# Queries and keys ordered by head, and differential scores over 64 rows of the array

## Chip, cores and metric

The kernel runs on one core of a Trainium2 chip. The metric is the device time of one execution in microseconds, the median of several runs. A profiled execution stands beside them; its times come from the hardware profiler.

## What is computed

A two-layer causal decoder trunk over 256 tokens of width 2048, in fp32. Layer 0 has a pooling mixer and a memory attention, then a squared-ReLU MLP. Then keys k1, k2 and values are made once from the residual stream, and layer 1 runs a differential attention with 12 heads: two query maps and two key maps of 64 channels for each head, and values of 128 channels.

```python
q1, q2 = (partial_rope(rms_norm(t, q_norm), cos, sin) for t in (q1, q2))   # (1, 256, 12, 64) each
a = softmax(mask(q1 @ k1.T * 64 ** -0.5)) - lam * softmax(mask(q2 @ k2.T * 64 ** -0.5))
o = a @ v                                                                  # a head: (256, 128)
token_out = rms_norm(o, subln_norm) * (1.0 - lam_init)
```

Beside it stand a memory attention of 4 heads of 128 channels, one output projection, and a second MLP.

## The kernel before

Activations lie with the channels on the 128 partitions, in 16 chunks (`NK`), and 256 tokens along the free dimension. Every large matmul is made in fp32r with operands split into a high and a low part. `Feed` brings the weights from DRAM in the order of their use, in blocks of 128x128, four to a "quad" of 512 columns. It loads them into `raw` (SyncE's queue), rounds a quad to its high part on ScalarE (`hi_ring<-raw`, L168) and takes the low part on VectorE (`lo_ring`, L169), three jobs ahead (`AHEAD`) of the matmul that needs it. The order is not written by hand: `program` is run twice, first dry, so that `Plan` collects the blocks in order, and then for real. The host lays the weights out in that order.

`b_tile` makes the query and key projections. For each of 16 chunks, `wide_step` takes one quad of 512 output columns and makes six matmuls (L449 to L451, three for each half of the tokens) with the tokens as rows of the result. After each wide step `tick()` runs what `at(d, fn)` put d ticks ahead; so the steps of the heads are laid between the projections' matmuls. The framework's scheduler then fixes each engine's order, and may shift an instruction against its neighbours.

A block of 128 columns is two heads of one map. The keys take `w_kv`'s blocks as they stand, six of map 0 and then six of map 1. The queries' chunk c, 512 columns of `w_in_q` as the host reorders them, has four heads: the first two heads' block of map 0 and of map 1, then the other two heads' blocks. `key_rows` and `query_rows` copy a projection out of PSUM (L490, L512), sum its squares by head, and `rope` turns the first 16 channels of each head in place. `turn_rows` transposes keys into `kT` (12 chunks of 128 x 256, six for each map, in the tile `big`). `turn_queries` transposes a pair of heads and evicts them (L1260) into two tiles of `qb`: in the first tile only partitions 0 to 63 are filled, in the second only 64 to 127. The rest was set to zero (L1249, L1250) once. So a score matmul can use all 128 rows of a key chunk, which holds two heads: the other head's 64 rows meet zeros.

`diff_head` is a head's attention, in four steps at ticks of their own:
- `scores`: for the second half of the queries (t = 1) both maps against 256 keys into `s1` (L1292), then for the first half both maps against 128 keys into `s0` (L1295). Both tiles are one PSUM bank of the tag "s", which has two. VectorE adds the causal mask (L1297, L1298), takes the maxima (L1302) and multiplies them by the row scales `y` (L1303). ScalarE makes the exponentials with their sums (L1306). VectorE combines the two maps into `a` (L1312 and the helper `stt`, L318).
- `turn`, four ticks later: three transposes of `a` (`dt`, L1321), and ScalarE's copy.
- `pv`: the product with the values (`do`, L1327 to L1329), its statistics and scale.
- `back`: transposes of the result (`o_t`, L1350) into `cat1`.

The heads of the last chunk run while `c_tile` makes the memory queries (`mq`, L429 to L431). The memory heads' scores use the same tag "s". The trace names the parts of one large tile alike: q, e, a and the rest are `att`, and `kT` and the values are `big`.

Of the kernel before, what the change touches and what calls it, by code (L numbers as in the profile page):

```python
# [9 lines left out]

F32 = mybir.dt.float32
F32R = mybir.dt.float32r
BF16 = mybir.dt.bfloat16
AF = mybir.ActivationFunctionType
ALU = mybir.AluOpType
AX = mybir.AxisListType
# [2 lines left out]
P = 128  # L19
# [86 lines left out]
class Feed:  # L106
# [119 lines left out]
    def quad(self, what):  # L226

        job = ("N", self.pos // 4)
        if self.dry:
            self.plan.entries.append(what)  # L230
            if self.pos % 4 == 0:
                self.plan.jobs.append(job)
            return Nothing(), Nothing()
        if self.pos % 4 == 0:
            self.fill(job)
        return self.split[job][:2]
# [44 lines left out]
def program(ctx, tc, plan, dry, xT, memT, par, lam, cst, wst, yT):  # L281
# [173 lines left out]
    def b_tile(ps, w, l, c, xs):  # L455
        for k in range(NK):
            wide_step(ps, (w, l, k, c, 4), xs, k)


    def rstd_from(name):  # L460
        st = stat("st_" + name)
# [22 lines left out]
    def key_rows(ps, cols, d):  # L484

        n = 512 // d
        raw = tp.tile([P, 2, 512], F32, tag="rows", bufs=3, name="krow")
        v = tp.tile([P, 2, n], F32, tag="w16", bufs=6, name="kv")
        for t in range(2):
            nc.scalar.activation(raw[:, t, :], ps[t], AF.Copy, scale=cols[0][:, t : t + 1])  # L490
            sq = tp.tile([P, 512], F32, tag="rowsq", bufs=1, name="ksq")
            nc.scalar.activation(sq, raw[:, t, :], AF.Square)
            nc.vector.tensor_reduce(
                out=v[:, t, :], in_=sq.rearrange("p (h d) -> p h d", d=d), axis=AX.X, op=ALU.add
            )
        v = v.rearrange("p t n -> p (t n)")
        nc.vector.tensor_scalar(out=v, in0=v, scalar1=1.0 / d, scalar2=EPS, op0=ALU.mult, op1=ALU.add)
        y = tp.tile([P, 2 * n], F32, tag="w16", bufs=6, name="ky")
        rsqrt_cols(y, v)
        for t in range(2):  # L500
            rows = raw[:, t, :].rearrange("p (h d) -> p h d", d=d)
            yb = y[:, t * n : t * n + n].unsqueeze(2).to_broadcast([P, n, d])
            nc.vector.tensor_mul(rows, rows, yb)
        return raw

    def query_rows(ps, cols, d):

        raw = tp.tile([P, 2, 512], F32, tag="rows", bufs=3, name="qrow")
        n = 512 // d
        v = tp.tile([P, 2 * n], F32, tag="w16", bufs=6, name="qv")  # L510
        for t in range(2):
            nc.scalar.copy(raw[:, t, :], ps[t])  # L512
            sq = tp.tile([P, 512], F32, tag="rowsq", bufs=1, name="qsq")
            nc.scalar.activation(sq, raw[:, t, :], AF.Square, scale=d ** -0.5)
            nc.vector.tensor_reduce(
                out=v[:, n * t : n * t + n], in_=sq.rearrange("p (h d) -> p h d", d=d),
                axis=AX.X, op=ALU.add,
            )
            nc.vector.tensor_scalar(
                out=v[:, n * t : n * t + n], in0=v[:, n * t : n * t + n],  # L520
                scalar1=cols[1][:, t : t + 1], scalar2=EPS, op0=ALU.mult, op1=ALU.add,
            )
        return raw, v
# [666 lines left out]
    at(12, lambda: c1.extend(columns("x")))  # L1190
    for c in range(3):
        ps = pair_of_banks(c, "k1")
        b_tile(ps, "w_kv", 0, c, x_kv)
        rows = key_rows(ps, c1, 64)
        rope(rows, ktab)
        for i in range(2):
            at(
                9,
                lambda i=i, c=c, rows=rows: turn_rows(
                    rows, 2 * i, kT[:, 4 * c + 2 * i : 4 * c + 2 * i + 2, :], gcol(G_KN)  # L1200
                ),
            )
# [40 lines left out]
    ab = [carve(384) for _ in range(2)]  # L1243
    aTb = [carve(384) for _ in range(2)]

    qb = [[carve(512).rearrange("p (m t) -> p m t", m=2) for _ in range(2)] for _ in range(3)]
    em1 = carve(512).rearrange("p (a t) -> p a t", a=2)
    for pair in qb:
        nc.vector.memset(pair[0][64:128], 0.0)  # L1249
        nc.vector.memset(pair[1][0:64], 0.0)  # L1250

    def turn_queries(rows, i, pair):
        t4 = pp.tile([P, 2, T], F32, tag="t", bufs=1, name="tq")
        for c in range(2):
            for t in range(2):
                nc.tensor.transpose(
                    t4[:, c, t * P : t * P + P], rows[:, t, (i + c) * P : (i + c) * P + P], ident
                )
        for g, r in enumerate((slice(0, 64), slice(64, 128))):
            nc.scalar.activation(pair[g][r], t4[r], AF.Copy, scale=qcol[r])  # L1260


    gsub = cp.tile([P, 1], F32, name="gsub")
    nc.vector.tensor_scalar_mul(gsub, gcol(G_SUB), 1.0 - LAM_INIT)
    idb = cp.tile([P, P], BF16, name="idb")
    nc.vector.tensor_copy(idb, ident)
    mkb = cp.tile([P, P], BF16, name="mkb")
    nc.vector.tensor_copy(mkb, const[:, C_MASK : C_MASK + P])

    def diff_head(h, q, y, lag, pv_lag, back_lag, by_pe):  # L1270

        j = h // 2
        e1, e0, a, aT = e1b[h % 2], e0b[h % 2], ab[h % 2], aTb[h % 2]
        yh = y.rearrange("p (t j m h) -> p t j m h", t=2, j=2, m=2)[:, :, j % 2, :, h % 2]
        ez = tp.tile([P, 2], F32, tag="ez", bufs=6, name="ez")

        def scores():
            s1 = pp.tile([P, 2, T], F32, tag="s", bufs=2, name="s1")
            s0 = pp.tile([P, 2, P], F32, tag="s", bufs=2, name="s0")
            if by_pe:  # L1280
                for m in range(2):
                    kk = kT[:, 6 * m + j, :]
                    nc.tensor.matmul(s1[:, m, :], q[:, m, P:T], kk, start=True, stop=False)
                    nc.tensor.matmul(s1[:, m, P:T], idb, mkb, start=False, stop=True)
                for m in range(2):
                    kk = kT[:, 6 * m + j, 0:P]
                    nc.tensor.matmul(s0[:, m, :], q[:, m, 0:P], kk, start=True, stop=False)
                    nc.tensor.matmul(s0[:, m, :], idb, mkb, start=False, stop=True)
            else:
                for m in range(2):  # L1290
                    kk = kT[:, 6 * m + j, :]
                    nc.tensor.matmul(s1[:, m, :], q[:, m, P:T], kk, start=True, stop=True)  # L1292
                for m in range(2):
                    kk = kT[:, 6 * m + j, 0:P]
                    nc.tensor.matmul(s0[:, m, :], q[:, m, 0:P], kk, start=True, stop=True)  # L1295
                mask = const[:, C_MASK : C_MASK + P].unsqueeze(1).to_broadcast([P, 2, P])
                nc.vector.tensor_add(s1[:, :, P:T], s1[:, :, P:T], mask)  # L1297
                nc.vector.tensor_add(s0, s0, mask)  # L1298
            mx = tp.tile([P, 2, 2], F32, tag="m4", bufs=6, name="mx")
            z = tp.tile([P, 2, 2], F32, tag="m4", bufs=6, name="z")  # L1300
            for t, s in ((1, s1), (0, s0)):
                nc.vector.tensor_reduce(out=mx[:, t, :], in_=s, axis=AX.X, op=ALU.max, negate=True)  # L1302
            nc.vector.tensor_mul(mx, mx, yh)  # L1303
            for t, s, e in ((1, s1, e1), (0, s0, e0)):
                for m in range(2):
                    nc.scalar.activation(  # L1306
                        e[:, m, :], s[:, m, :], AF.Exp, bias=mx[:, t, m : m + 1],
                        scale=yh[:, t, m : m + 1], accum_out=z[:, t, m : m + 1],
                    )

            zr = tp.tile([P, 2], F32, tag="m2", bufs=12, name="zr")
            nc.vector.reciprocal(zr, z[:, :, 1])  # L1312
            stt(zr, zr, nlam, z[:, :, 0], ALU.mult, ALU.mult)
            stt(ez, z[:, :, 0], EPS, z[:, :, 0], ALU.mult, ALU.mult)
            for t, e, dst in ((1, e1, a[:, P : P + T]), (0, e0, a[:, 0:P])):
                stt(dst, e[:, 1, :], zr[:, t : t + 1], e[:, 0, :], ALU.mult, ALU.add)
# [7 lines left out]
        def pv():  # L1324
# [3 lines left out]
            nc.tensor.matmul(o[:, 1, :], aT[:, P:T], vv[:, 0, hs], start=True, stop=False)  # L1328
            nc.tensor.matmul(o[:, 1, :], aT[:, T : T + P], vv[:, 1, hs], start=False, stop=True)  # L1329
            osb = vt("osb").rearrange("p (a b) -> p a b", a=2)  # L1330
            if by_pe:
                nc.vector.tensor_copy(osb, o)
                o = osb
            ss = tp.tile([P, 2], F32, tag="m2", bufs=12, name="o_ss")
            junk = vt("o_sq")
            for t in range(2):
# [21 lines left out]

    for c in range(3):
        ps = pair_of_banks(0, "q1")  # L1360
        b_tile(ps, "w_in_q", 1, c, x_mx)
        rows, v = query_rows(ps, c1, 64)
        rope(rows, qtab)
        y = query_scale(v, c1)
        for i in range(2):
# [3 lines left out]
            for g in range(2):  # L1369
                h = 2 * i + g  # L1370

                diff_head(
                    2 * j + g, q[g], y, 6 + 4 * h, *((8, 4 if c == 0 else 3) if c < 2 else (7, 3)), False
                )
    pT1 = tp.tile([P, 2, T], F32R, tag="acc2", bufs=1, name="pT1")
    pT1_lo = tp.tile([P, 2, T], F32R, tag="rowsq", bufs=1, name="pT1_lo")
# [101 lines left out]
```

## Time and profile before

| | |
|---|---|
| median of 3 runs | 2037.37 us (2037.07 to 2037.41) |
| profiled execution | 2036.78 us, its span 2035.0 us |
| TensorE matmuls busy | 2030.0 us, 11068 records |
| VectorE / ScalarE busy | 1722.7 / 1352.4 us |
| granted TensorE clock | 1.000 |
| HBM read | 386.54 MB, 191 GB/s over the span |

The span runs from the first to the last instruction; the profiled execution's own time has 1.78 us around it. A matmul's record lasts from its start until its result is written, so records overlap; how fast they follow each other is seen from their ends, as in the chain of waits. PE names the matmuls, PEld the weight loads, DVE is VectorE and ACT is ScalarE.

### The profile page before, as it was taken

The page shows a single profiled execution, that of the slowest core. Times are in us where ns is not written, and L with a number is a line of the kernel's source. Part 1 is how long each engine was busy: PE and PEld are TensorE (multiplying, and loading weights), DVE is VectorE, ACT ScalarE, POOL GpSimd, SP SyncE. Part 2 cuts the span into 40 slices and gives each one's busy share as a digit, 9 for nine tenths or more (in the row PEclk, how much of TensorE's full clock was granted, in tenths as well). Part 3 has the DMA queues.
Part 4 walks back from the last instruction along what each step waited for, and adds up shares of the span by engine and source line. Part 5 has one row for each costly group of instructions (what it writes and reads, how often), then busy time and mean ns, then how long its engine had stood idle before and what let it go on. Part 6 is the DMA issues. An engine that isn't in the chain of part 4 may idle for free.

```text
span 2035.0 us, 32279 instructions
## 1 busy us (share of the span) xinstructions
PE 2030.0 (100%) x11068; PEld 1753.2 (86%) x11068; DVE 1722.7 (85%) x3226; ACT 1352.4 (66%) x2520; POOL 54.5 (3%) x67
## 2 busy tenths in 40 slices
PE   9999999999999999999999999999999999999999
PEld 8888888888888888888888889888888888888888
DVE  8888889889879878999766788989879978988997
ACT  7765577666656756778665688566667656766764
POOL 0001300000000000000000000410000000000000
PEclk9999999999999999999999999999999999999999
DMA  9566556555555555645565434556555555555564
GB/s 317 167 200 191 189 177 203 190 197 197 187 202 201 186 205 193 212 168 186 189 227 195 166 125 140 192 177 204 189 197 197 186 202 195 188 208 200 195 205 134
DMA packets 110630, 390.75 MB, mean 192 GB/s; under 512 B 12544, under 2 KB 15232, under 8 KB 110464
## 3 DMA queue, kind: packets, MB, share of 16 engines
q1 hardware_dynamic: 110240, 388.61, 56.6%
q8 instruction: 86, 1.41, 0.3%
q14 instruction: 80, 0.66, 0.1%
q10 hardware_dynamic: 224, 0.07, 0.0%
HBM read 386.54 MB, written 2.10 MB: 191 GB/s over the span
## 4 chain that ended last, share of the span: by engine, by line
PE 99%; DMA 0%; DVE 0%; SPq 0%; ACT 0%; issue 0%; ACTq 0%
PE x_bank L415 33%; PE x_bank L417 16%; PE wo L415 6%; PE p L798 5%; PE p L799 5%; PE p L800 5%; PE wo L417 3%; PE u L415 2%; PE ff L415 2%; PE u L417 1%; PE q L449 1%; PE q L451 1%; PE k L449 1%; PE q L450 1%; PE k L450 1%; PE v L450 1%
## 5 line engine op out<-in xcount | busy, mean ns | idle before, releaser
L168 ACT CAST hi_ring<-raw 128x512 fp32r<-128x512 f32 x1193 | 736.0, 620 | 513.8 <-PE x_bank L415 303.3
L169 DVE TENSOR_TENSOR lo_ring<-raw,hi_ring 128x512 fp32r<-128x512 f32 x1193 | 817.7, 696 | 187.9 <-ACT hi_ring L168 149.3
L415 PE MATMUL x_bank<-fx,hi_ring 128*128 128x512 f32 x1920 | 602.2, 395 | 0.0
L417 PEld LDWEIGHTS x_bank<-fx,lo_ring 128*128 128x128 f32 x1920 | 361.1, 188 | 83.5
L417 PE MATMUL x_bank<-fx,lo_ring 128*128 128x256 f32 x1920 | 377.5, 278 | 0.0
L415 PEld LDWEIGHTS x_bank<-fx,hi_ring 128*128 128x128 f32 x1920 | 301.4, 189 | 9.3
L415 PE MATMUL x_bank<-z,hi_ring 128*128 128x512 f32 x960 | 301.1, 395 | 0.0
L169 DVE TENSOR_TENSOR lo_ring<-slab,hi_ring 128x1024 fp32r<-128x1024 f32 x188 | 230.0, 1224 | 54.5 <-ACT hi_ring L168 53.7
L168 ACT CAST hi_ring<-slab 128x1024 fp32r<-128x1024 f32 x188 | 196.8, 1047 | 73.3 <-PE x_bank L415 36.4
L417 PEld LDWEIGHTS x_bank<-z,lo_ring 128*128 128x128 f32 x960 | 180.5, 188 | 41.7
L417 PE MATMUL x_bank<-z,lo_ring 128*128 128x256 f32 x960 | 188.8, 278 | 0.0
L415 PE MATMUL wo<-cat,hi_ring 128*128 128x512 f32 x512 | 162.5, 398 | 0.0
L415 PEld LDWEIGHTS x_bank<-z,hi_ring 128*128 128x128 f32 x960 | 151.9, 189 | 6.4 <-ACT room L722 0.4
L417 PEld LDWEIGHTS wo<-cat,lo_ring 128*128 128x128 f32 x512 | 95.6, 188 | 20.9
L722 ACT COPY room<-x_bank 128x512 f32<-128x512 f32 x180 | 104.8, 582 | 2.0 <-PE x_bank L417 2.0
L417 PE MATMUL wo<-cat,lo_ring 128*128 128x256 f32 x512 | 102.5, 280 | 0.0
L798 PE MATMUL p<-hi_ring,sit 128*128 128x512 f32 x256 | 100.5, 393 | 0.0
L799 PE MATMUL p<-hi_ring,sit 128*128 128x512 f32 x256 | 100.2, 392 | 0.0
L800 PE MATMUL p<-lo_ring,sit 128*128 128x512 f32 x256 | 99.7, 390 | 0.0
L767 ACT ACTIVATE room<-room 128x256 f32<-128x256 f32 x128 | 53.2, 415 | 41.2 <-DVE room L318 40.9
L415 PEld LDWEIGHTS wo<-cat,hi_ring 128*128 128x128 f32 x512 | 79.0, 189 | 1.3 <-DVE cat L318 0.4
L798 PE MATMUL p<-hi_ring,z 128*128 128x512 f32 x192 | 75.2, 392 | 0.0
(336 smaller groups left out, 3128.0 us busy)
## 6 DMA issues: line engine op xcount, KB each, us to landing
raw<-in_w SPq DMA_DIRECT2D x595, 512.0 KB, 3.9
slab<-in_w SPq DMA_DIRECT2D x124, 512.0 KB, 3.5
memraw<-in_mem SPq DMA_DIRECT2D x5, 512.0 KB, 3.9
resid<-in_x SPq DMA_DIRECT2D x8, 256.0 KB, 5.5
room<-in_w SPq DMA_DIRECT2D x4, 512.0 KB, 4.6
out_y<-resid SPq DMA_DIRECT2D x15, 128.0 KB, 1.9
memraw<-in_mem SPq DMA_DIRECT2D x5, 256.0 KB, 5.7
raw<-in_w SPq DMA_DIRECT2D x3, 256.0 KB, 3.2
```

The lines of the kernel that those rows point to most:

```text
L168: self.last_cast = self.nc.scalar.copy(hi, src)
L169: low = self.nc.vector.tensor_sub(lo, src, hi.bitcast(F32))
L415: nc.tensor.matmul(ps, hi, xs[:, k, :], start=first and c == 0, stop=False)
L417: nc.tensor.matmul(ps[:, T : 2 * T], lo, xs[:, k, 0:T], start=False, stop=last and c == len(ks) - 1,)
L449: nc.tensor.matmul(ps[t], x[t][1], hi, start=k == 0, stop=False)
L450: nc.tensor.matmul(ps[t], x[t][0], hi, start=False, stop=False)
L451: nc.tensor.matmul(ps[t], x[t][0], lo, start=False, stop=k == NK - 1)
L722: nc.scalar.copy(x, ps)
L767: at(3, lambda: nc.scalar.activation(stage[i % 8], y[:, 0:T], AF.Square))
L798: nc.tensor.matmul(ps, a[1], hi, start=first, stop=False)
L799: nc.tensor.matmul(ps, a[0], hi, start=False, stop=False)
L800: nc.tensor.matmul(ps, a[0], lo, start=False, stop=last)
```

## The change

Blocks of weights for queries and keys are taken in another order: a chunk of 512 columns now has the four heads of map 0 in its first half and those of map 1 in the second (`map_tile` in place of `b_tile`). The copy out of PSUM writes the rows by head: 64 channels of map 0, then 64 of map 1, so that a block of 128 columns is one head with both its maps. The keys' chunk h is then head h, map 0 in partitions 0 to 63 and map 1 in 64 to 127, and so are the queries; the zero halves go, with their zeroing and with one of the two evictions of a pair.

The scores are matmuls over 64 rows, from partition 0 for map 0 and from partition 64 for map 1. Their order takes turns between the maps. The PSUM tiles are now one for each map, with three blocks of 128 columns: the first half of the queries in block 0, the second half in blocks 1 and 2. Masks and maxima go by map. The maximum comes in three columns, and one more small operation joins two of them. The branch `by_pe`, which no call used, goes with its two constants.

```diff
+    def map_tile(ps, w, l, blocks, xs):
+        for k in range(NK):
+            wide_step(ps, [(w, l, k, n, 1) for n in blocks], xs, k)
+
+    def by_head(row, d):
+        return row if d == P else row.rearrange("p (h m d) -> p m h d", m=2, d=d)
+
+    def by_map(row, d):
+        return row if d == P else row.rearrange("p (m h d) -> p m h d", m=2, d=d)
...
-            nc.scalar.copy(raw[:, t, :], ps[t])
+            nc.scalar.copy(by_head(raw[:, t, :], d), by_map(ps[t], d))
...
-        b_tile(ps, "w_kv", 0, c, x_kv)
+        map_tile(ps, "w_kv", 0, (2 * c, 2 * c + 1, 6 + 2 * c, 7 + 2 * c), x_kv)
...
-    qb = [[carve(512).rearrange("p (m t) -> p m t", m=2) for _ in range(2)] for _ in range(3)]
+    qb = [carve(512).rearrange("p (c t) -> p c t", c=2) for _ in range(3)]
-    for pair in qb:
-        nc.vector.memset(pair[0][64:128], 0.0)
-        nc.vector.memset(pair[1][0:64], 0.0)
...
-        for g, r in enumerate((slice(0, 64), slice(64, 128))):
-            nc.scalar.activation(pair[g][r], t4[r], AF.Copy, scale=qcol[r])
+        nc.scalar.activation(q, t4, AF.Copy, scale=qcol)
...
-            s1 = pp.tile([P, 2, T], F32, tag="s", bufs=2, name="s1")
-            s0 = pp.tile([P, 2, P], F32, tag="s", bufs=2, name="s0")
...
-                for m in range(2):
-                    kk = kT[:, 6 * m + j, :]
-                    nc.tensor.matmul(s1[:, m, :], q[:, m, P:T], kk, start=True, stop=True)
-                for m in range(2):
-                    kk = kT[:, 6 * m + j, 0:P]
-                    nc.tensor.matmul(s0[:, m, :], q[:, m, 0:P], kk, start=True, stop=True)
-                mask = const[:, C_MASK : C_MASK + P].unsqueeze(1).to_broadcast([P, 2, P])
-                nc.vector.tensor_add(s1[:, :, P:T], s1[:, :, P:T], mask)
-                nc.vector.tensor_add(s0, s0, mask)
+            s = [pp.tile([P, 3, P], F32, tag="s", bufs=2, name=f"s{m}") for m in range(2)]
+            for m, t in ((0, 0), (1, 1), (0, 1), (1, 0)):
+                r = slice(64 * m, 64 * m + 64)
+                nc.tensor.matmul(
+                    s[m][:, t : 2 * t + 1, :], q[r, t * P : t * P + P], kT[r, h, 0 : t * P + P],
+                    start=True, stop=True,
+                )
+            mask = const[:, C_MASK : C_MASK + P].unsqueeze(1).to_broadcast([P, 2, P])
+            mx3 = tp.tile([P, 2, 3], F32, tag="m6", bufs=4, name="mx3")
+            for m in range(2):
+                nc.vector.tensor_add(s[m][:, 0:3:2, :], s[m][:, 0:3:2, :], mask)
+                nc.vector.tensor_reduce(
+                    out=mx3[:, m, :], in_=s[m], axis=AX.X, op=ALU.max, negate=True
+                )
+            nc.vector.tensor_tensor(
+                out=mx3[:, :, 1], in0=mx3[:, :, 1], in1=mx3[:, :, 2], op=ALU.min
+            )
-            for t, s in ((1, s1), (0, s0)):
-                nc.vector.tensor_reduce(out=mx[:, t, :], in_=s, axis=AX.X, op=ALU.max, negate=True)
-            nc.vector.tensor_mul(mx, mx, yh)
+            nc.vector.tensor_mul(mx, mx3[:, :, 0:2].rearrange("p m t -> p t m"), yh)
...
-        b_tile(ps, "w_in_q", 1, c, x_mx)
+        map_tile(ps, "w_in_q", 1, (4 * c, 4 * c + 2, 4 * c + 1, 4 * c + 3), x_mx)
```

More of the change, by code (lines that the diff above doesn't have):

```diff
@@ L12 @@
 F32R = mybir.dt.float32r
-BF16 = mybir.dt.bfloat16
 AF = mybir.ActivationFunctionType
@@ L229, in quad @@
         if self.dry:
-            self.plan.entries.append(what)
+            self.plan.entries += what if isinstance(what, list) else [what]
             if self.pos % 4 == 0:
@@ L489, in key_rows @@
         for t in range(2):
-            nc.scalar.activation(raw[:, t, :], ps[t], AF.Copy, scale=cols[0][:, t : t + 1])
+            nc.scalar.activation(
+                by_head(raw[:, t, :], d), by_map(ps[t], d), AF.Copy, scale=cols[0][:, t : t + 1]
+            )
             sq = tp.tile([P, 512], F32, tag="rowsq", bufs=1, name="ksq")
@@ L1244, in program, with turn_queries @@
     aTb = [carve(384) for _ in range(2)]
-    qb = [[carve(512).rearrange("p (m t) -> p m t", m=2) for _ in range(2)] for _ in range(3)]
+    qb = [carve(512).rearrange("p (c t) -> p c t", c=2) for _ in range(3)]
     em1 = carve(512).rearrange("p (a t) -> p a t", a=2)
-    for pair in qb:
-        nc.vector.memset(pair[0][64:128], 0.0)
-        nc.vector.memset(pair[1][0:64], 0.0)
-    def turn_queries(rows, i, pair):
+    def turn_queries(rows, i, q):
         t4 = pp.tile([P, 2, T], F32, tag="t", bufs=1, name="tq")
@@ L1258, in turn_queries @@
                 )
-        for g, r in enumerate((slice(0, 64), slice(64, 128))):
-            nc.scalar.activation(pair[g][r], t4[r], AF.Copy, scale=qcol[r])
+        nc.scalar.activation(q, t4, AF.Copy, scale=qcol)
     gsub = cp.tile([P, 1], F32, name="gsub")
     nc.vector.tensor_scalar_mul(gsub, gcol(G_SUB), 1.0 - LAM_INIT)
[L1265 to L1268, printed above, removed]
@@ L1270, in diff_head @@
-    def diff_head(h, q, y, lag, pv_lag, back_lag, by_pe):
-        j = h // 2
+    def diff_head(h, q, y, lag, pv_lag, back_lag):
         e1, e0, a, aT = e1b[h % 2], e0b[h % 2], ab[h % 2], aTb[h % 2]
-        yh = y.rearrange("p (t j m h) -> p t j m h", t=2, j=2, m=2)[:, :, j % 2, :, h % 2]
+        yh = y.rearrange("p (t h m) -> p t h m", t=2, m=2)[:, :, h % 4, :]
         ez = tp.tile([P, 2], F32, tag="ez", bufs=6, name="ez")
         def scores():
-            s1 = pp.tile([P, 2, T], F32, tag="s", bufs=2, name="s1")
-            s0 = pp.tile([P, 2, P], F32, tag="s", bufs=2, name="s0")
-            if by_pe:
-                for m in range(2):
-                    kk = kT[:, 6 * m + j, :]
-                    nc.tensor.matmul(s1[:, m, :], q[:, m, P:T], kk, start=True, stop=False)
-                    nc.tensor.matmul(s1[:, m, P:T], idb, mkb, start=False, stop=True)
-                for m in range(2):
-                    kk = kT[:, 6 * m + j, 0:P]
[L1287 to L1295, printed above, removed]
-                mask = const[:, C_MASK : C_MASK + P].unsqueeze(1).to_broadcast([P, 2, P])
-                nc.vector.tensor_add(s1[:, :, P:T], s1[:, :, P:T], mask)
-                nc.vector.tensor_add(s0, s0, mask)
@@ L1299, in scores @@
+            for m in range(2):
[5 more added lines that the diff above has]
+                out=mx3[:, :, 1], in0=mx3[:, :, 1], in1=mx3[:, :, 2], op=ALU.min
+            )
             mx = tp.tile([P, 2, 2], F32, tag="m4", bufs=6, name="mx")
+            nc.vector.tensor_mul(mx, mx3[:, :, 0:2].rearrange("p m t -> p t m"), yh)
@@ L1300, in scores @@
             z = tp.tile([P, 2, 2], F32, tag="m4", bufs=6, name="z")
-            for t, s in ((1, s1), (0, s0)):
-                nc.vector.tensor_reduce(out=mx[:, t, :], in_=s, axis=AX.X, op=ALU.max, negate=True)
-            nc.vector.tensor_mul(mx, mx, yh)
-            for t, s, e in ((1, s1, e1), (0, s0, e0)):
+            for t, e in ((1, e1), (0, e0)):
                 for m in range(2):
                     nc.scalar.activation(
-                        e[:, m, :], s[:, m, :], AF.Exp, bias=mx[:, t, m : m + 1],
+                        e[:, m, :], s[m][:, t : 2 * t + 1, :].rearrange("p a b -> p (a b)"), AF.Exp, bias=mx[:, t, m : m + 1],
@@ L1330, in pv @@
             osb = vt("osb").rearrange("p (a b) -> p a b", a=2)
-            if by_pe:
-                nc.vector.tensor_copy(osb, o)
-                o = osb
             ss = tp.tile([P, 2], F32, tag="m2", bufs=12, name="o_ss")
@@ L1372, in program @@
                 diff_head(
-                    2 * j + g, q[g], y, 6 + 4 * h, *((8, 4 if c == 0 else 3) if c < 2 else (7, 3)), False
+                    2 * j + g, q[:, g, :], y, 6 + 4 * h, *((8, 4 if c == 0 else 3) if c < 2 else (7, 3))
                 )
```

## The prediction, on record before the result

> **What bounds the kernel now.** I read the page first, then the busy time by stage, then the chain of waits around one head's scores.
>
> ```profile
> span 2035.0 us, 32279 instructions
> PE 2030.0 (100%) x11068; PEld 1753.2 (86%) x11068; DVE 1722.7 (85%) x3226; ACT 1352.4 (66%) x2520; POOL 54.5 (3%) x67
> PE 99%; DMA 0%; DVE 0%; SPq 0%; ACT 0%; issue 0%; ACTq 0%
> ...
> core 0: us, PE busy (x) PEld busy (x) DVE busy (x) ACT busy (x) POOL busy (x), PEclk, DMA share, GB/s
> ...
> 1149.00:1205.00 56.00, 56.00 (x306) 48.08 (x305) 46.25 (x149) 45.55 (x137) 0.00 (x0) 1.00 0.40 131
> 1205.00:1260.00 55.00, 54.97 (x418) 52.22 (x417) 49.24 (x170) 48.56 (x155) 0.00 (x0) 1.00 0.39 129
> ```
>
> TensorE is busy for 2030.0 of 2035.0 us and is 99% of the chain that ended last. The second view is the stage that the change is about, 1149 to 1260 us: TensorE idles there for 0.03 us in all, at a granted clock of 1.00. So the program's time is TensorE's list of instructions, and an edit counts only if it makes that list shorter or longer, or if it makes TensorE wait. VectorE (46.25 of 56, then 49.24 of 55) and ScalarE (45.55, 48.56) are over 80% busy here, so a wait is not far off.
>
> **The scores on TensorE.** One head, in the chain of waits:
>
> ```profile
> 1165.11 0.33 PE dt L1321 x3
> 1165.44 0.87 PE s L1292 x4
> 1166.30 0.45 PE s L1295 x4
> 1166.75 0.23 PE q L449
> 1166.98 0.23 PE q L450
> ...
> L1292 PEld LDWEIGHTS s<-big,att x48: 188/191/193, 1149.6 to 1245.8; 128*128 128x128 f32 x48
> L1292 PE MATMUL s<-big,att x48: 377/379/383, 1149.9 to 1246.1; 128*128 128x256 f32 x48
> ...
> L1295 PEld LDWEIGHTS s<-big,att x48: 187/192/193, 1150.5 to 1250.5; 128*128 128x128 f32 x48
> L1295 PE MATMUL s<-big,att x48: 270/275/351, 1150.7 to 1250.6; 128*128 128x128 f32 x48
> ```
>
> Columns of the first rows are start, length, line. The two fp32 matmuls of 256 columns (L1292) leave four records in 0.87 us, the two of 128 columns (L1295) four in 0.45: each fp32 matmul runs as two records, each with its own weight load. A head's scores cost 0.87 + 0.45 = 1.32 us, and twelve heads 15.8 us, 0.78% of the program. Half of each array pass multiplies zeros, since 64 of q's 128 rows are the other head's.
>
> After the change the eight records stay, with the same columns, but each uses 64 rows, and the rows take turns: map 0 (128 columns), map 1 (256), map 0 (256), map 1 (128). If different halves run at once, the bound is half of 1.32, or 0.66. Nearer is the weight load, which the change does not shorten in columns:
>
> ```profile
> 1226.31 0.65 PE s L1292 x3
> 1226.95 0.34 PE st_mq L596 x4
> ...
> 1229.55 0.52 PE s L1295 x4
> ```
>
> L596 multiplies 128x128 weights by only two columns, and its records still end 0.11 us apart (0.34 us in three steps; the first ends with the record before it). So loads pass at one per 0.11 us, and eight take 0.88 us. I take 0.88, because every row here has loads in line: a gain of 1.32 - 0.88 = 0.44 us for a head whose four matmuls stand together. The ends are 0 (the halves run in line) and 0.66.
>
> They do not stand together in all heads. The order on an engine is laid by the framework's scheduler, and before the change five of the twelve heads have something between their score matmuls (the heads scored at 1197.82, 1215.30, 1225.92, 1235.51 and 1245.41); the rows of the first and the last:
>
> ```profile
> 1197.82 0.60 PE L1292 MATMUL s<-big,att 128*128 128x256 f32 x2
> 1198.39 0.52 PE L1321 MATMUL dt<-const,att 128*128 128x128 f32 x3
> 1198.75 0.60 PE L1292 MATMUL s<-big,att 128*128 128x256 f32 x2
> ...
> 1245.41 1.03 PE L1292 MATMUL s<-big,att 128*128 128x256 f32 x4
> ...
> 1250.28 0.61 PE L1295 MATMUL s<-big,att 128*128 128x128 f32 x4
> ```
>
> In the last three heads L1295 comes only 3 to 5 us after L1292, because by the code the memory heads' scores take their turn on the two banks of tag "s". The new code asks for the same two banks, one for each map, so there map 0 would run alone and map 1 later. I count 7 whole heads: 7 x 0.44 = **3.1 us gained**.
>
> **Going in and out of half height.** No row of before has a matmul over 64 rows, so what it costs to change between 128 rows and 64 is not shown. Lower end: 0. From fp32 scores to the fp32r projection (1166.30 to 1166.75) the stream goes on without a step, 0.23 us for the first record as for the next; a gain is excluded, as a change of form can do no work. Upper end: nothing is hidden over a change. A 256-column record lasts 379 ns while its successor starts 0.87/4 = 0.22 us later, so its last 0.16 us pass under the next; a load lasts 0.19 us and is also hidden now. Bare, one after the other, that is 0.35 us. I take 0.19: the array must be clear of full-height work before half of it is another array, so tail and load stand open, but side by side, the longer setting the time. Whole heads have 2 changes, broken ones 4: 7 x 2 + 5 x 4 = 34, x 0.19 = **6.5 us lost** (0 to 11.9). The Trainium skill's page "TensorEngine Tiling (Array Packing)", section "Key Properties", says that going to another tiling mode, not just to another tile, drains TensorE. It gives no figure and no run here shows it; by it the sum is the one made here, and by the row at 1166.75 alone it would be 6.5 us lower.
>
> **The softmax behind the scores.** VectorE's work for a head:
>
> ```profile
> L1302 DVE TENSOR_REDUCE mx<-s 128x2 f32<-128x512 f32 x12 | 8.2, 684 | 0.0
> L1302 DVE TENSOR_REDUCE mx<-s 128x2 f32<-128x256 f32 x12 | 5.0, 420 | 0.0
> L1303 DVE TENSOR_TENSOR mx<-mx,qy 128x4 f32<-128x4 f32 x12 | 1.9, 160 | 0.1
> ...
> 1171.46 0.17 DVE L1312 RECIPROCAL zr<-z 128x2 f32<-128x2 f32 x1 [0.28 <-ACT att L1306]
> 1171.67 0.22 DVE L318 SCALAR_TENSOR_TENSOR zr<-zr,nlam,z 128x2 f32<-128x2 f32 x1
> 1171.92 0.75 DVE L318 SCALAR_TENSOR_TENSOR att<-att,zr 128x256 f32<-128x256 f32 x2
> ...
> 1172.82 0.52 PE L1321 MATMUL dt<-const,att 128*128 128x128 f32 x3
> ...
> 1181.71 0.74 DVE L318 SCALAR_TENSOR_TENSOR att<-att,zr 128x256 f32<-128x256 f32 x2
> ...
> 1182.66 0.49 PE L1321 MATMUL dt<-const,att 128*128 128x128 f32 x3
> ...
> 1197.50 0.75 DVE L318 SCALAR_TENSOR_TENSOR att<-att,zr 128x256 f32<-128x256 f32 x2
> ```
>
> The two reduces become two of 384 elements, (684 + 420)/2 = 552 ns each: no change in sum. The mask adds keep 256 elements each. New is one minimum of two columns, like L1303: 160 ns, 12 x 0.16 = 1.9 us of VectorE, none of it TensorE's. But the chain gets longer: the minimum itself, one more dependent step (0.21 us from start to start in the rows at 1171.46 and 1171.67), and the first mask add now needs the third matmul and not the second. Before, it started when L1292's four records were done, 0.45 us ahead of the scores' end; the last matmul alone is 2 x 0.11 = 0.22, so it moves 0.23 us closer. Together some 0.4 us later. While VectorE waits for it, subtractions into lo_ring (L169) stand behind it; they are made three jobs ahead, three wide steps of 3 x 0.23 us x 2, which covers 0.4 us. Who waits is dt, four steps on: the rows show `a` ready at 1171.92 + 0.75 = 1172.67 and dt at 1172.82, and at 1198.25 against 1198.39. Those two heads have no slack, a third (1182.45 against 1182.66) has 0.2. So 0.4 + 0.4 + 0.2 = **1.0 us lost** (0 if the scheduler's order or ScalarE's relief below takes it up, 2.6 if four more heads lose 0.4 too).
>
> **What costs nothing.** ScalarE, VectorE and the loads:
>
> ```profile
> L1260 ACT ACTIVATE att<-tq,qcol x12: 681/682/687, 1147.3 to 1223.7; 64x512 f32<-64x512 f32 x12
> L512 ACT COPY qrow<-q 128x512 f32<-128x512 f32 x6 | 3.5, 590 | 0.9 <-PE q L451 0.9
> L1249 DVE MEMSET att<- x3: 485/485/485, 1075.4 to 1079.7; 64x512 f32 x3
> ```
>
> Twelve evictions of q at 0.68 us become six over 128 rows: 4.1 us off ScalarE, priced at 0 as TensorE waits for none of them; it could take back part of the 1.0. The six zeroings (0.49 us each at 1075 us), and two casts of constants that only an unused branch read, lay under TensorE's work and go. The copies of q and k rows write the same 512 elements in runs of 64; if that slowed them by as much again (0.59 us), it would be 3.5 us over q on an engine 20% idle, ahead of turns that come 4 steps later. The weights' blocks come from DRAM in the same number and size, one of 512 columns being four of 128; no DMA moves past another, and neither SP's nor POOL's queue changes. The exponentials keep count and shape, transposes and the products with v too.
>
> **Sum.** -3.1 + 6.5 + 1.0 = +4.4 us. The profiled execution took 2036.78 us with a span of 2035.0, 0.59 below the median of 2037.37; the difference goes onto the median: **2041.8 us**. About 0.2% (4.07 us) is what a measurement of this kernel can tell from no change, and this lies just above it.
>
> **Rivals.** *The turns pay* (faster). If entering half height is as free as entering fp32r, the term of 6.5 goes: -3.1 + 1.0 = -2.1, or 2035.3 us. With all twelve heads kept together -5.3 + 1.0 = -4.3, and with loads of the two halves side by side, 0.66 us a head, -7.9 at most: 2029.5 to 2035.3. It decides from a change cost under 0.09 us (3.1/34). For it: nothing in the profile costs a step between forms. Against: every one of these forms uses all rows. The Trainium skill's page "TensorE: Matmul & The Clock Gate", part 3, has row groups run at once, with starts 4 ns apart; no run here shows it, and it would take this rival to its lower end.
>
> *In line and with changes* (slower still). The halves don't overlap, since each fp32 matmul is two records on one half, and changes cost 0.19: 6.5 + 1.0 = +7.5, 2044.9 us; at 0.35 it is 2050.3. For it: records end strictly one after the other in every row.
>
> *Nothing happens on TensorE*: no overlap and no cost, 15.8 us as before, and only the chain's 1.0: 2038.4 us. For it: a matmul's time here goes by columns, not by rows.
>
> **Numbers.** Forecast 0.42, the turns pay 0.28, in line 0.20, nothing 0.10. The forecast's own range, 0.16 to 0.30 us for a change, is 2040.7 to 2045.5; 0.30 of its 0.42 is slower by over 0.2%, 0.12 within. Of the turns, 0.18 is faster, 0.10 within; in line 0.19 slower, 0.01 within; nothing 0.09 within, 0.01 slower. That makes faster 0.18, same 0.32, slower 0.50. The range leaves out the turns' lower end and bare changes in line: 2033 to 2047 us.
>
> **What would show it.** Score records on 64 rows; their eight ends within 0.9 us in whole heads (right), 1.3 (in line); a step of 0.19 us before the first score record and before the record after the last one, against none (the turns). Heads in one piece should be seven. dt's wait for `a` should grow by up to 0.4 us in the tight heads; q's eviction should be six of 0.68. The prediction is wrong if a change shows under 0.09 us or over 0.35, or if TensorE waits elsewhere for longer than 3 us.

## The result

| | median us | range, runs |
|---|---|---|
| before | 2037.41 | 2037.07 to 2038.51, 15 |
| changed | 2041.93 | 2041.25 to 2042.5, 15 |

The ratio is 1.0021, with a 95% interval of 1.0014 to 1.0029: the change made the kernel 4.5 us slower. The forecast was 2041.8. Its sum came out almost exactly, but not its terms, as the profile shows. The page of the changed kernel:

```profile
span 2040.3 us, 32289 instructions
PE 2032.5 (100%) x11068; PEld 1747.2 (86%) x11068; DVE 1722.0 (84%) x3230; ACT 1348.5 (66%) x2514; POOL 54.8 (3%) x67
PE 98%; ACT 1%; DVE 0%; DMA 0%; issue 0%; SPq 0%
```

The same 11068 records on TensorE, four instructions more on VectorE and six fewer on ScalarE. TensorE is still the chain. The timeline of TensorE gives the place, from the first score to the second MLP's first product `p`; before, then the changed kernel:

```profile
1149.86 1.02 PE L1292 MATMUL s<-big,att 128*128 128x256 f32 x4
...
1363.97 0.40 PE L798 MATMUL p<-hi_ring,z 128*128 128x512 f32 x1
```

```profile
1150.93 0.92 PE L1283 MATMUL s<-big,att 64*128 64x128 f32 x8
...
1369.23 0.40 PE L811 MATMUL p<-hi_ring,z 128*128 128x512 f32 x1
```

This stretch takes 214.11 us before and 218.30 after, 4.2 more. The other 1.1 us of the two profiled executions lie ahead of the first score. Nothing shows that they are part of the change: the control `before_turn_later` below, with before's code but for one tick, has its first score at 1150.73, and `full_rows`, with the changed layout, at 1149.97. What follows the stretch is equal within 0.1 us.

Inside it, the chain of waits around one whole head, and one that `dt` cuts in two (start, length, line):

```profile
1150.78 0.23 PE q L450
1151.00 0.85 PE s L1283 x6
1151.86 0.43 PE q L448
1152.29 0.23 PE q L449
...
1165.88 0.22 PE do L1325 x2
1166.11 0.41 PE s L1283 x2
1166.52 0.50 PE dt L1317 x3
1167.02 0.85 PE s L1283 x6
1167.87 0.43 PE q L448
```

The whole head's eight records (the chain names six, as it follows one at a time) end within 0.85 us, against 1.32 before. Ahead of the first there is a step: it ends 0.30 us after the record before it, where a record of 128 columns takes 0.11, so 0.19 us stand open. The row at 1166.11 shows the same: two records of 128 columns take 0.41 there, and 0.22 without a step. Then the first q record takes 0.43 and not 0.23: 0.20 us on leaving. So the head costs 0.66 + 0.19 + 0.20 = 1.05 us, a gain of 0.27. The second head costs 0.41 + 0.85 for its scores, and the steps behind them are 0.50 - 0.33 = 0.17 on dt and 0.20 on q: 1.63 us, a loss.

The step on leaving follows the weight load of the next record:

```profile
L1283 PEld LDWEIGHTS s<-big,att x96: 182/186/188, 1150.9 to 1256.7; 64*128 64x128 f32 x96
...
L1343 PEld LDWEIGHTS o_t<-const,osb x24: 137/140/143, 1176.0 to 1279.1; 128*128 128x128 f32 x24
```

A load lasts 0.19 us for scores and q, 0.14 for transposes, and the step is 0.19 to 0.20 and 0.15 (before o_t) in turn. So the step goes with the load; that nothing else of about the same length sets it is not shown.

Adding up the ends of all records in the stretch: the 96 score records take 10.9 us net of the first step of each piece, not 15.8 (**-4.9**). They stand in 20 pieces (a piece is a run of score records with nothing between them), so there are 40 changes of height, from 128 rows to 64 or back: 3.9 us going in and 3.4 going out (**+7.3**). What is left of the 4.3 us that the stretch grew by its ends is **+1.9**, waits and small gaps. The largest waits in the chain by releaser:

```profile
PE s L1283 <- ACT att L641: 0.4, 1, 0.4
PE dt L1317 <- DVE o_v L317: 0.4, 1, 0.4
PE dt L1317 <- DVE att L317: 0.3, 1, 0.3
PE o_t L1343 <- DVE osb L1338: 0.2, 1, 0.2
```

Before, the same question has no answer in this stretch. The columns are the sum, how often, and the longest. These make 1.3 of the 1.9 us; the rest the view does not name. The first line is a score that waits for the bank of a memory head's scores until its exponentials (L641) are made. The second is put down to `o_v`, a small operation that VectorE made right behind `a`.

### The profile page after: what moved, and what is told of

It is laid out like the page before. It is cut to its first block, busy times and chain, and to the rows that moved or that the text cites. A ratio compares the mean times of both kernels' runs of the same rounds, so it can differ in the third digit from the quotient of the medians.

```text
span 2040.3 us, 32289 instructions
## 1 busy us (share of the span) xinstructions
PE 2032.5 (100%) x11068; PEld 1747.2 (86%) x11068; DVE 1722.0 (84%) x3230; ACT 1348.5 (66%) x2514; POOL 54.8 (3%) x67
## 4 chain that ended last, share of the span: by engine, by line
PE 98%; ACT 1%; DVE 0%; DMA 0%; issue 0%; SPq 0%
PE x_bank L414 33%; PE x_bank L416 16%; PE wo L414 6%; PE p L811 5%; PE p L812 5%; PE p L813 5%; PE wo L416 3%; PE u L414 2%; PE ff L414 2%; PE u L416 1%; PE k L448 1%; PE v L448 1%; PE k L449 1%; PE k L450 1%; PE v L449 1%; PE v L450 1%
```

## The experiments

Two theories stood against each other. **Height**: TensorE pays for each change between 128 and 64 rows, and gets part of it back where halves run at once. **Waits**: the longer softmax chain costs the time. Each group below shares its runs of the kernel before (2037.19, 2037.28, 2037.26 and 2037.02 us).

**Full height in the new layout.**

```diff
...
-                    s[m][:, t : 2 * t + 1, :], q[r, t * P : t * P + P], kT[r, h, 0 : t * P + P],
+                    s[m][:, t : 2 * t + 1, :], q[:, m, t * P : t * P + P], kT[:, h, 0 : t * P + P],
...
```

> The changed kernel, but with score matmuls over all 128 rows: queries again in two tiles with a zero half (two evictions of a pair, six zeroings), everything else as changed (rows by head, a bank per map, order of the turns, maxima by map). Theory (height): what the change cost in its stage, 4.2 us by the traces, is +7.3 for 40 changes between 128 and 64 rows, -4.9 for halves that run at once, and +1.9 for longer waits. Here the first two go: 2041.9 - 2.4 = 2039.5 us, no record before or after a score stands alone. Rival (waits): the loss is the longer softmax chain, and stays: 2041.9 us or a little more, as ScalarE has its 4.1 us of evictions back.

2038.91 us, ratio 1.0008 (0.9999 to 1.0017). Against its own runs of before that is 1.7 us above, where the changed kernel stood 4.5 above: going back to 128 rows takes 2.8 us away, 0.4 more than the sum had it. The rival would have kept 2041.9. The 1.7 us that stay are at the edge of what can be told: the interval reaches from 0.2 us below before to 3.5 above. The chain of waits around a head that dt cuts:

```profile
1157.42 0.66 PE s L1286 x4
1158.08 0.06 issue
1158.14 0.52 PE dt L1320 x3
1158.65 0.66 PE s L1286 x4
1159.31 0.23 PE q L448
```

Both pieces take 0.66, the 1.32 of before, and q follows at 0.23 at once: no step, in or out. What remains, the 1.7 us, is not of height; dt's 0.52 in place of 0.33, with 0.06 ahead of it, is a wait for `a`. (The built order has 24 pieces here, and they cost no step.)

**The height alone.** In the kernel before, one small matmul behind each of 48 wide steps of the value projection:

```diff
-        b_tile(ps, "w_kv", 0, 3 + c, x_kv)
+        extra = pp.tile([P, 2], F32, tag="st", bufs=1, name="extra")
+        for k in range(NK):
+            wide_step(ps, ("w_kv", 0, k, 3 + c, 4), x_kv, k)
+            nc.tensor.matmul(extra, ones_d[0:64], ones_d[0:64, 0:2], start=True, stop=True)
```

The other probe has `0:128` in place of `0:64`.

> The kernel before, with one small fp32 matmul (weights 128x128 of a constant, two columns) behind each of the 48 wide steps of the value projection, into a bank that is free there; its result is not read. All 128 rows. Both theories: two records at 0.11 us each, 48 x 0.22 = 10.6 us more: 2047.8 us.

> The same small matmul over the first 64 rows only (weights 64x128, two columns). Theory (height): going from 128 rows to 64 and back costs 0.19 + 0.20 us on top, whatever is multiplied: 48 x 0.39 = 18.7 us more than the probe over 128 rows, 2066 us. Rival (waits: the steps around the scores are waits for operands or banks, not the height): nothing here is waited for, so the same as over 128 rows, 2048 us.

2048.64 us (ratio 1.0056, 1.0042 to 1.0069) over 128 rows and 2062.89 us (1.0126, 1.0112 to 1.014) over 64. The chain of waits, 64 rows and then 128:

```profile
1030.15 0.23 PE v L451
1030.38 0.31 PE extra L1208 x2
1030.69 0.43 PE v L449
1031.12 0.23 PE v L450
```

```profile
1031.07 0.23 PE v L451
1031.31 0.12 PE extra L1208 x2
1031.43 0.34 PE v L449
1031.77 0.23 PE v L450
```

The same step as in the scores, with nothing to wait for: 0.31 - 0.12 = 0.19 going in, and v's next record 0.43 in place of 0.23, 0.20 going out. That falsifies the rival for this term. The difference is 14.3 us, 0.30 for each pair of changes and not 0.39, and the run over 64 rows stays 3 us under the 2066 expected: with two columns the 128-row probe cannot cover the next load either, and its v record pays 0.34 - 0.23 = 0.11 of it. I had missed that. By these rows the pair costs 0.39 - 0.11 = 0.28.

**Order of the score matmuls.**

```diff
-            for m, t in ((0, 0), (1, 1), (0, 1), (1, 0)):
+            for m, t in ((0, 0), (0, 1), (1, 1), (1, 0)):
```

> The changed kernel with the four score matmuls in another order: both of map 0, then both of map 1, instead of taking turns. Theory (height, halves overlap when neighbours in the queue lie on different halves): a record on the same half has to wait for the one before it, so only map 0's last record and map 1's first overlap; a head in one piece takes 1.1 us and not 0.66, and the kernel 2 to 3 us more: 2044 to 2045 us. Rival (the overlap is only how records are written down, and the time is by columns): no change, 2041.9 us.

2043.61 us, ratio 1.0033 (1.0021 to 1.0046): 6.4 us above before and not 4.5, so 1.9 more, just under the expected 2 to 3. (The two intervals overlap; by the traces the stretch is 2.0 us longer.) But the reason was wrong. A whole head and a cut one in its chain of waits:

```profile
1150.68 0.86 PE s L1283 x6
1151.54 0.43 PE q L448
...
1157.72 0.85 PE s L1283 x4
1158.57 0.48 PE dt L1317 x3
1159.05 0.85 PE s L1283 x4
```

The whole head takes 0.86 us without turns as with them. In strict order map 1 could start only with map 0's last record, and the head would take 1.1 us or more. The starts show it too. These records start in the head's first 0.03 us:

```profile
L1283 PE MATMUL s<-big,att x2: 373/426/480, 1150.6 to 1150.6; 64*128 64x128 f32 x1, 64*128 64x256 f32 x1
```

In the built order the four matmuls stand as written, with map 0's 128 columns first, and a matmul leaves two records. So in that order the first two records would both have 128 columns; the second one here has 256. Read as map 1's first, it has gone past map 0's second, which waits for its half. So a half takes its next matmul past those that wait for the other half, and turns are not needed within a piece. The cut head loses, because dt now parts the maps: each piece has one half only, 0.85 us twice.

**The turn one tick later**, in the changed kernel and, as control, in the kernel before:

```diff
-        at(lag + 4, turn)
+        at(lag + 5, turn)
```

> The changed kernel with the turn of a head one tick later (lag + 5, not lag + 4), so that its transposes no longer share a tick with the next head's scores. In the built order the scores stand in 16 pieces and not in 20, 8 heads whole and not 4. Theory (height): 8 changes fewer at 0.18 us are -1.5; four more heads whole gain some 0.2 each by overlap, -0.8; waits of the transposes for a go, about -1.3: 2038.3 us. Rival (waits alone cost): -1.3, 2040.6 us.

> The kernel before with the same one tick for the turn: the control of the run with the turn later. Scores are over 128 rows, so pieces cost nothing; only its own waits for a, 0.3 us by the trace, can go. Both theories: 2037.0 to 2037.4 us. If it gains over 1 us, the tick itself is worth that, whatever the rows.

2038.48 us (0.9998 to 1.0016 of before), and 2036.89 us for the control (0.999 to 1.0008). Measured against before, 1.3 us and not 4.5: the edit is worth 3.2 us with 64 rows, and 0.3 with 128. The interval of the first includes before's time. The waits of dt are gone from the answer, and so is the score's for L641:

```profile
PE o_t L1343 <- DVE osb L1338: 0.2, 1, 0.2
```

Pieces fell from 20 to 16. The scores with their changes, and the waits that stand among them, fell from 19.0 to 16.5 us, still above 15.8, and the four heads that stay in two pieces are the reason. One that the product with v cuts:

```profile
1180.64 0.91 PE s L1283 x4
1181.55 0.42 PE do L1323 x2
1181.96 0.22 PE do L1324 x2
1182.19 0.22 PE do L1325 x2
1182.41 0.85 PE s L1283 x4
1183.26 0.37 PE o_t L1343 x2
```

0.91 + 0.85 for the pieces, and 0.42 - 0.22 and 0.37 - 0.22 behind them: 2.1 us, twice a whole head.

**All heads whole**, by a bank of the projections' tag for map 1 of the last four heads, and its control:

```diff
+            tags = (("s", 2), ("mm", 3) if h >= 8 else ("s", 2))
...
-        at(lag + 4, turn)
+        at(lag + 5, turn)
...
-        ((8, 4 if c == 0 else 3) if c < 2 else (7, 3))
+        ((9, 3) if c < 2 else (7, 3))
```

> The changed kernel with the turn one tick later, the product with v one tick later in the first two chunks (9, the result's turn 3 behind it), and map 1's scores of the last four heads in a bank of tag mm: in the built order eleven heads are whole and one is in two pieces (13 pieces, 26 changes). Theory (height): 12 x 0.66 + 13 x 0.38 + some 0.2 for the cut head = 13.1 us in place of 15.8, and the waits as in the kernel before with the later turn: 2036.9 - 2.7 = 2034.2 us, below the kernel before. Rival (64 rows cost something beyond the changes, or the ticks bring new waits): not below 2036.9.

> The kernel before with the same ticks and with s0 of the last four heads in a bank of tag mm: the control. Scores over 128 rows cost the same in any pieces: 2036.9 us as with the later turn alone, within 0.5.

2042.62 us (1.0015 to 1.0036) and 2041.9 us for the control (1.0014 to 1.0032): a miss for both, as the control alone is 4.6 us above before, where the later turn alone was 0.3 below. In whole_a, the waits and the busy time by stage:

```profile
PE wo L414 <- ACT att L1306: 4.2, 2, 2.7
...
core 0: us, PE busy (x) PEld busy (x) DVE busy (x) ACT busy (x) POOL busy (x), PEclk, DMA share, GB/s
...
1235.00:1240.00 5.00, 3.22 (x27) 3.02 (x26) 4.87 (x19) 3.97 (x16) 0.00 (x0) 1.00 0.30 103
1240.00:1245.00 5.00, 4.13 (x17) 3.85 (x18) 1.85 (x7) 4.02 (x17) 0.00 (x0) 0.51 0.31 108
1245.00:1250.00 5.00, 5.00 (x29) 4.07 (x28) 2.58 (x12) 2.30 (x8) 0.00 (x0) 0.81 0.16 55
```

The output projection needs these banks and waits 4.2 us for exponentials. The scores with their changes did fall, to 13.8 us with the waits among them, near the 13.1 expected. But the gain drowns in the new waits and in the slower clock behind them (0.51 and then 0.81, where the control has 1.00): an estimate from these rows, 0.49 of 4.13 us busy and 0.19 of 5.00, is 3 us for the clock in this execution. So the times of this pair don't decide between the theories.

**64 rows only where heads stand whole.** The first eight heads over 64 rows, all in one piece; the last four over 128 rows with zero halves:

```diff
+                qq = q[r] if h < 8 else q[:, m]
+                kk = kT[r if h < 8 else slice(0, P), h, 0 : t * P + P]
...
-        at(lag + pv_lag, pv)
+        at(lag + pv_lag + (h in (2, 3)), pv)   # with the turn at lag + 5
```

> The changed kernel with the turn one tick later, the product with v one tick later for heads 2 and 3 alone, and scores over 64 rows for the first eight heads only, all of which stand in one piece in the built order. The last four heads, whose two banks come apart, have 128 rows with zero halves; all banks are of tag s. Theory (height): eight heads at 0.66 + 0.19 + 0.18 = 1.03 us and not 1.32, -2.3 against the kernel before with the later turn (2036.9): 2034.6 us, below the kernel before; new waits may take up to 1 us of it. Rival (64 rows never pay, the gain is eaten by waits): 2036.9 or above.

2037.2 us, ratio 1.0 (0.9991 to 1.0009): not the 2034.6 expected, and no faster than before or than the control; in the time the rival is right. In the trace the scores with their changes take 14.5 us, 1.3 below the control, and waits and small gaps are 1.6 above it. So the gain of height is there, and is eaten.

**What the other waits are.**

> The changed kernel with score matmuls over all 128 rows and the turn one tick later. If the 1.7 us by which the full-row version lies above the kernel before are waits of the turn for a, behind the longer chain of the maxima, they go: 2037.0 to 2037.4 us. If they come from the layout, the copies by head or the banks by map, they stay: 2038.9 us.

2039.35 us, ratio 1.0011 (1.0002 to 1.002). The time did not fall, though dt's waits are gone from the trace as in the changed kernel with the later turn: others stand in their place. The longest wait of TensorE that is left, in the chain:

```profile
1252.72 1.16 ACT att L641 x4
1253.88 0.04 issue
1253.92 0.92 PE s L1286 x4
```

A score waits for a memory head's exponentials, as in the changed kernel. If the banks are held too long by exponentials that go by token half, an order by map should help:

```diff
-            for t, e in ((1, e1), (0, e0)):
-                for m in range(2):
+            for m in range(2):
+                for t, e in ((1, e1), (0, e0)):
```

> Scores over 128 rows and the later turn, as in the run that kept 2039.35 us, with one edit: the exponentials go by map (both of map 0, then both of map 1), so that map 0's bank is free after two of them and not after three. If its 2.4 us over the control (2036.9) are waits for the two banks of tag s, held longer by banks by map, this takes a good part back: 2038.0 to 2038.5 us. If not, 2039.3 us.

> The version with 64 rows for the first eight heads alone (2037.2 us) with the same edit, exponentials by map. By its trace, waits stand 1.3 us above those of the control with the later turn, and TensorE's scores with their changes 1.3 us below. If the banks are what is waited for, some 0.5 to 1.0 us go: 2036.2 to 2036.7 us, just below the kernel before; if not, 2037.2 us.

2039.34 us (1.0003 to 1.0021) and 2040.02 us (1.0006 to 1.0023): no help, and in the mixed version 3 us worse, where the built order also has three pieces more. In the first of the two the wait that the edit was aimed at did go (the last head's score piece takes 0.65 us and not 0.92), and another came, 0.3 us before a memory head's product. So this theory fell: taking one wait away does not bring its time back here. Which part of the change makes the last 2 us of waits (banks by map, the longer chain of the maxima, or the order that the scheduler then finds) stays open.

## Why the prediction came out

**Right: where the time is decided.** TensorE's list and its waits hold all of it. The relief of ScalarE (six evictions of 0.69 us and not twelve of 0.68) and the zeroings brought nothing visible, and q's copy by head measured 587 ns against 590.

**Right: the price of a change of height**, 0.19 us in and 0.15 to 0.20 out where 0.19 was taken. Of the reason given, the longer of tail and load, the steps before transposes (0.15 with a load of 0.14) support the load; the tail's part is not shown. The drain that the Trainium skill's page "TensorEngine Tiling (Array Packing)", section "Key Properties", states agrees with the trace, which has a step of 0.15 to 0.20 us at the changes. That the size is one weight load each way comes from the runs.

**Wrong, for the good: the overlap.** The sum had eight loads in line, 0.88 us a head, and the bound 0.66 as the far end. Measured was 0.66, in every whole head: loads of the two halves pass side by side. And the sum gave nothing to a cut head, where pieces with both halves overlap too. The gain was 4.9 us, where 3.1 stood: 2.6 in the four whole heads, the rest in the cut ones.

**Wrong, for the bad: how many heads stay whole.** Seven were counted from the order before, four were. dt fell into five heads, where it had stood in three, and the banks part three more, as forecast. That made 40 changes and not 34, 7.3 us and not 6.5. (The order before gives 36 by the prediction's own way of counting, since the head scored at 1235.51 stood in three pieces there.)

**Too small: the waits**, 1.9 and not 1.0 us. Of these, dt's waits behind `a` (0.7 us) are named by the trace and go with a later turn. A score's wait for a bank that memory heads share (0.4) and one of `o_t` (0.2) were not in the sum; the remaining 0.6 is not traced to a cause.

So two errors of opposite sign, 1.8 us of gain too little and 1.7 of loss too little, hid each other: that the sum came within 0.2 us is luck. The price of a change of height is not. The rival in which the turns pay needed a change under 0.09 us and fell by the probe. The one without overlap fell by the whole head's 0.66, and the one in which nothing happens with both.

## What to carry to other kernels

Half-height matmuls between full-height work pay by the piece: here 0.34 to 0.39 us for each entry and exit together, against 0.66 us saved in a head of 1.32. Before using them, count the pieces in the built order, not the matmuls in the source, and lay other work of the same engine elsewhere. And when a sum comes out, check its terms, for errors can cancel.

## What was not expected of the hardware

The two halves of the array load weights and take matmuls independently: a whole head ends in 0.66 us in both orders tried, where eight loads at one per 0.11 us would take 0.88. The Trainium skill's page "TensorE: Matmul & The Clock Gate", part 3, has matmuls start and end strictly in program order; the run without turns, 0.86 us for a whole head with the step in, and a record of 256 columns among its first two, speaks against it for matmuls of different halves.

In whole_a the granted clock was 0.51 over the 5 us from 1240, in which TensorE's longest wait, 2.7 us, ends. In the control, with a longest wait of 1.7 us in the same 5 us, it was 1.00. If the wait set the clock back, it cost more than itself; no run isolates that.
